# Modulation vectors finished four accumulators at a time instead of two, with six accumulator buffers

## The chip, the cores and the metric

The kernel runs on one core of one Trainium2 chip. The metric is the device time of one execution in microseconds (us); of several runs the median is given. The profiled execution is one further run of the same program.

## The reference

Two layers of a hybrid diffusion backbone run over 256 latent and 256 context tokens with 1024 channels. Each layer normalises its input, projects it into a short convolution, a Fourier mixer, an attention and three gates, merges the three branches, projects the sum, and adds a squared-ReLU MLP. Every normalised input and every residual is scaled by modulation vectors, which come from the conditioning vector `c` (latents) and `c_ctx` (context):

```python
for l in range(DEPTH):
    mod = (silu(c) @ w_mod[l] + b_mod[l])[:, None, :]            # 6 parts of 1024 numbers
    mod_c = (silu(c_ctx)[None] @ w_mod[l] + b_mod[l])[:, None, :]
    sh1, sc1, gt1, sh2, sc2, gt2 = split(mod, 6)
    h = modulate(x, g_norm1[l], sh1, sc1)                       # rms_norm(x, g) * (1 + scale) + shift
    z = h @ w_in[l]
    ...                                                         # convolution, Fourier, attention
    x = x + gt1 * merge_branches(z, ...)
    x = x + gt2 * sq_relu_mlp(modulate(x, g_norm2[l], sh2, sc2), w_ff1[l], w_ff2[l])
    # layer 0 does the same for the context tokens with mod_c
```

All inputs, weights and outputs are float32. `w_mod` is 2 x 1024 x 6144.

## The kernel before

**Matrix products.** Activations lie transposed: channels on the 128 partitions, tokens along the row (512 in layer 0, latents and context together; 256 in layer 1). Weights come in chunks of 1024 x 256 (`fetch`, line 384, one DMA from the queue of SP into one of two `raw` buffers). Each half of a chunk is split into a rounded part `whi` (cast on ACT, line 362) and a rest `wlo` (subtraction on DVE, line 363), four buffers each. `fm` (line 414) makes three matmuls per pair of tiles: high by high (line 437), low by high (440), high by low (442). One chunk of layer 0 is 48 matmuls with 512 columns and fills two of the four PSUM banks of the pool `mm`. A new chunk takes the two banks that are used longest ago, and can start when those have been read.

**The modulation vectors.** Parts 0 and 1 of layer 0 are computed at the start (`mod_start`) and aren't touched by the change. All others are side work that runs between the big products. `mod_loads` (line 270) loads `w_mod` in pieces of 256 rows x 512 columns into one of two `modr` buffers. `mod_steps` (line 312) multiplies each of 128 rows per partition by its number of `silu(c)` and adds it to an accumulator `acc` of 128 x 512 on DVE (line 327 the first time, then 329): eight such additions for one half part (512 of a part's 1024 columns) and one stream. In layer 0, and for parts 0 and 1 of layer 1, there are two streams (latent and context), so a half part fills two accumulators; for parts 2 to 5 of layer 1 it fills one.

What is left is a sum over the 128 partitions, which `mod_finish` (line 280) makes on TensorE when two accumulators are full. Four matmuls with 32 columns of ones as weights (line 286) each take 256 columns of an accumulator and write to a strip of 32 partitions of one PSUM tile. They are plain float32, of which the trace shows two records each. ACT copies the tile to SBUF (line 291), two transposes (line 296, of 128 x 128) bring the sums onto the partitions, and two small additions on DVE (line 299) add the bias and write `modT`. There are 16 such finishes.

**The order of the work.** `mod_steps` is a generator that is advanced one step at a time by `fm` (`mods.tick`, line 444), at a rate set per stage (`RATES`, line 35). Inside `mod_finish` it lets W1 steps pass ahead of the matmuls and W2 ahead of the transposes. `mod_need` (line 308) runs it on until a part is there, ahead of the code that uses the part: parts 2, 3 and 4 at the output projection (stage `wo`), part 5, which is the gate `gt2` of the MLP's residual, after the first block of hidden units in stage `ff`. From the program so recorded, a scheduler makes the order of each engine's instructions by a simulated timeline. Some instructions (`keep_in_program_order`) keep their order among themselves. The engines then run their lists in order and wait for each other by semaphores.

Stages are named in the tiles: `init`, `n1`, `u`, `conv`, `fou`, `qkv`, `gate` (with the attention beside it), `ag`, `wo`, `ff`, each for layer 0 and 1. A tile `ffL_mm` is a bank of stage `ff`, `ffL_acc` an accumulator made there (the norm's sum of squares has the name `acc` too, lines 158 to 163). `residual` (line 452) reads a bank, multiplies it by `gt` from `modT`, and adds it to `xT` on DVE (line 455).

Of the kernel before, what the change touches and what calls it, by code (L numbers as in the profile page):

```python
# [8 lines left out]
F32 = mybir.dt.float32  # L9
F32R = mybir.dt.float32r  # L10
AF = mybir.ActivationFunctionType
ALU = mybir.AluOpType
# [3 lines left out]
P = 128  # L16
D = 1024
KT = D // P
# [12 lines left out]
NT0 = 2  # L31
MLAG = 1
LAG = 2
W1, W2 = 3, 2
RATES = [0.6, 1.3, 0.4, 0.8]
AR = [1.3, 0.8]

# [2 lines left out]
def hybrid_block_kernel(  # L40
# [7 lines left out]
    nc = tc.nc  # L48
# [13 lines left out]
    pmod = ctx.enter_context(tc.tile_pool(name="pmod", bufs=1, space=PSUM))  # L62
# [4 lines left out]
    def nm(s):  # L67
        uid[0] += 1
        return f"{stage[0]}_{s}_{uid[0]}"
# [4 lines left out]
    def scratch(shape=(P, 512), dt=F32):  # L74
        return scr.tile(list(shape), dt, tag="scr", name=nm("scr"))

    def small(shape, tag, dt=F32, bufs=4):
        return tiny.tile(shape, dt, tag=tag, name=nm(tag), bufs=bufs)
# [4 lines left out]
    def aux(shape=(P, 512)):  # L83
        return paux.tile(list(shape), F32, tag="aux", name=nm("aux"))
# [34 lines left out]
    ones = const.tile([P, P], F32, tag="ones", name="ones")  # L119
# [7 lines left out]
    prm = []  # L127
# [103 lines left out]
    modT = [const.tile([P, 48, 2], F32, tag=f"modT{l}", name=f"modT{l}") for l in range(DEPTH)]  # L231
# [38 lines left out]
    def mod_loads(todo):  # L270
        for l, j, ns in todo:
            for h in range(2):
                for k2 in range(KT // 2):
                    r = tiny.tile([P, 2, 512], F32, tag="modr", name=nm("modr"), bufs=2)
                    c0 = j * D + h * 512
                    nc.sync.dma_start(r, w_mod[l, k2 * 256 : (k2 + 1) * 256, c0 : c0 + 512]
                                      .rearrange("(k p) n -> p k n", p=P))
                    yield l, j, ns, h, k2, r

    def mod_finish(accs, dsts, l):  # L280

        ps = pmod.tile([P, 256], F32, tag="mod", name=nm("mod"))
        for _ in range(W1):
            yield
        for g in range(4):
            tc.keep_in_program_order(PE.matmul(
                ps[32 * g : 32 * g + 32, :], ones[:, 0:32],
                accs[g // 2][:, (g % 2) * 256 : (g % 2 + 1) * 256], start=True, stop=True,
            ))
        sb = scratch()[:, :256]  # L290
        A.copy(sb, ps)
        for _ in range(W2):
            yield
        tp = aux((P, 2, P))
        for e in range(2):
            tc.keep_in_program_order(PE.transpose(tp[:, e, :], sb[:, e * P : (e + 1) * P], ident))
        tv = tp.rearrange("p e (g r) -> p g e r", r=32)[:, :, :, 0]
        for i, (f, s) in enumerate(dsts):
            V.tensor_tensor(
                modT[l][:, f : f + 4, s].rearrange("p (g e) -> p g e", e=2),  # L300
                tv[:, 2 * i : 2 * i + 2, :],
                prm[l][:, f : f + 4].rearrange("p (g e) -> p g e", e=2), op=ALU.add,
            )
        yield

    ready = set()
# [5 lines left out]
    def mod_steps(todo):  # L312
        loads = mod_loads(todo)
        cur = next(loads, None)
        accs, dsts = [], []
        while cur is not None:
            l, j, ns, h, k2, r = cur
            cur = next(loads, None)
            if k2 == 0:
                for s in range(ns):  # L320
                    accs.append(small([P, 512], "acc", bufs=2))
                    dsts.append((j * 8 + h * 4, s))
            for kk in range(2):
                for s in range(ns):
                    a, w = accs[s - ns], cs2[:, s, 2 * k2 + kk : 2 * k2 + kk + 1]
                    if k2 + kk == 0:
                        v = V.tensor_scalar(a, r[:, kk, :], w, None, op0=ALU.mult)
                    else:
                        v = V.scalar_tensor_tensor(a, r[:, kk, :], w, a, op0=ALU.mult, op1=ALU.add)  # L329
                    tc.keep_in_program_order(v)  # L330
                    yield
            if k2 == KT // 2 - 1 and len(accs) == 2:
                yield from mod_finish(accs, dsts, l)
                accs, dsts = [], []
                if h == 1:
                    ready.add((l, j))


    class Side:
# [3 lines left out]
        def set(self, gen, rate):  # L343
            self.gen, self.rate, self.due = gen, rate, 0.0
# [167 lines left out]
    for l in range(DEPTH):  # L512
# [3 lines left out]
        T = ns * S  # L516
# [115 lines left out]
        for tt in range(nt):  # L632
            ps = aux((P, 2, 256))
# [17 lines left out]
        for ft in range(2):  # L651
            ps = aux()
# [108 lines left out]
        for ci, c0 in ((2, OFF_K), (0, OFF_Q), (1, OFF_Q + 256)):  # L761
            ch = plain(w_in[l], 0, c0, (V, G) if last else (V, V)).prep()
            for tt in range(4 if ci == 2 else nt):
                ps = bank((P, 256))
# [126 lines left out]
        for j in range(4):  # L891
# [5 lines left out]
            for o in range(2):  # L897
                f = 2 * j + o
# [42 lines left out]
        acc = accs(streams)  # L941
# [4 lines left out]
        rbc = []  # L946
# [9 lines left out]

        def norm2(s, rb, todo):
            if last:
                rbc.append(small([P, 512], "acc", bufs=2)[:, :T])
                A.copy(rbc[0], rb)  # L960
                return
            modulate(hh2, hl2, todo, {s: rb}, gn2, sh2)

        project(lambda j: plain(w_o[l], 0, j * 256), msrc, gt1, acc, norm2)


# [25 lines left out]
        for b in range(nblk):  # L992
# [40 lines left out]
            if nr == 1:  # L1033
                if final and not last:
                    mods.drain()
                    acc = accs(streams)
# [88 lines left out]
```

## Time and profile before

| | before |
|---|---|
| median of 3 runs | 1148.34 us (1147.14 to 1148.45) |
| the profiled execution, its own time | 1147.6 us |
| span of the profiled execution | 1145.7 us |
| TensorE (PE), busy | 1123.6 us, 98% |
| DVE, busy | 779.8 us, 68% |
| ACT, busy | 503.2 us, 44% |
| DMA, all queues | 180.02 MB, mean 157 GB/s |

The 1.9 us between the profiled execution's time and its span lie before the first and after the last instruction. PE is busy nearly throughout. PE's matmuls overlap: one starts every 0.23 us and lasts 0.39, so that the distance from one start to the next, not the duration, says what a matmul costs. PEld is the queue of the weight loads, one ahead of each matmul; in brackets stands how long PE or PEld was idle ahead of a row, and for whom.

### The profile page before, as it was taken

The numbers are of one execution on the slowest core, as the hardware profiler recorded it, in microseconds if no ns is written. First come the engines' busy times: TensorE is split into PE (matmuls) and PEld (weight loads), VectorE is DVE, ScalarE is ACT, GpSimd is POOL, SyncE is SP. The second block draws the span as 40 slices with busy tenths as digits, with TensorE's granted clock in tenths as the row PEclk, the third lists the DMA queues.
The fourth block names the chain that finished last, engine by engine and source line by source line (L and its number), as shares of the span: only waits on it lengthen the run. The fifth ranks groups of instructions, "written<-read, shape, count | busy, mean of one in ns | idle before, by whom it ended". The sixth has DMA issues, their size and how long they took to land.

```text
span 1145.7 us, 17784 instructions
## 1 busy us (share of the span) xinstructions
PE 1123.6 (98%) x7083; PEld 980.9 (86%) x7083; DVE 779.8 (68%) x1434; ACT 503.2 (44%) x884; POOL 59.1 (5%) x57
## 2 busy tenths in 40 slices
PE   6999999999999999999999999999999999999998
PEld 4689888887787998878888888899999999988986
DVE  4677776577878876766656664678886567756754
ACT  4245444443332454243234135245666456754652
POOL 2102100000000100000000000033300000000000
PEclk9999999999999999999999999999999999999999
DMA  9923322234755253655456664525434565555553
GB/s 291 293 90 98 93 92 82 86 110 120 205 172 184 82 173 115 198 174 178 130 177 208 206 209 141 198 78 167 147 111 130 137 202 178 182 184 184 184 184 110
DMA packets 156764, 180.02 MB, mean 157 GB/s; under 512 B 5229, under 2 KB 126473, under 8 KB 156681
## 3 DMA queue, kind: packets, MB, share of 16 engines
q1 hardware_dynamic: 156680, 178.88, 49.9%
q8 instruction: 56, 0.92, 0.3%
q14 instruction: 28, 0.22, 0.1%
HBM read 177.81 MB, written 1.05 MB: 156 GB/s over the span
## 4 chain that ended last, share of the span: by engine, by line
PE 90%; SPq 3%; DMA 3%; DVE 2%; ACT 1%; POOL 0%; issue 0%; DVEq 0%; ACTq 0%
PE ffL_mm L437 12%; PE ffL_mm L440 12%; PE ffL_mm L442 12%; PE gateL_mm L437 5%; PE gateL_mm L440 5%; PE gateL_mm L442 5%; PE agL_mm L440 3%; PE agL_mm L437 3%; PE agL_mm L442 3%; PE ffL_mm L1070 3%; PE ffL_mm L1071 3%; PE ffL_mm L1069 3%; SPq L468 2%; PE woL_mm L440 2%; PE woL_mm L442 2%; PE woL_mm L437 2%
## 5 line engine op out<-in xcount | busy, mean ns | idle before, releaser
L362 ACT CAST ffL_whi<-ffL_raw 128x1024 fp32r<-128x1024 f32 x128 | 134.4, 1052 | 217.9 <-PE ffL_mm L442 164.1
L363 DVE TENSOR_TENSOR ffL_wlo<-ffL_raw,ffL_whi 128x1024 fp32r<-128x1024 f32 x127 | 155.2, 1222 | 100.4 <-ACT ffL_whi L362 100.2
L437 PE MATMUL ffL_mm<-woL_big,ffL_whi 128*128 128x258 f32 (+2 forms) x544 | 171.1, 329 | 0.0
L440 PE MATMUL ffL_mm<-woL_big,ffL_wlo 128*128 128x258 f32 (+2 forms) x544 | 170.5, 327 | 0.0
L442 PE MATMUL ffL_mm<-woL_big,ffL_whi 128*128 128x258 f32 (+2 forms) x544 | 133.2, 328 | 0.0
L437 PEld LDWEIGHTS ffL_mm<-woL_big,ffL_whi 128*128 128x128 f32 x544 | 103.0, 190 | 10.2 <-issue 1.6
L440 PEld LDWEIGHTS ffL_mm<-woL_big,ffL_wlo 128*128 128x128 f32 x544 | 103.1, 190 | 8.9 <-issue 0.4
L329 DVE SCALAR_TENSOR_TENSOR ffL_acc<-ffL_modr,cs,ffL_acc 128x512 f32<-128x512 f32 x126 | 90.5, 748 | 25.6 <-DMA ffL_modr<-in_w_mod_dram 24.6
L437 PE MATMUL ffL_mm<-ffL_big,ffL_whi 128*128 128x512 f32 (+1 forms) x288 | 105.3, 368 | 0.0
L440 PE MATMUL ffL_mm<-ffL_big,ffL_wlo 128*128 128x512 f32 (+1 forms) x288 | 104.9, 367 | 0.0
L442 PEld LDWEIGHTS ffL_mm<-woL_big,ffL_whi 128*128 128x128 f32 x544 | 91.0, 190 | 8.7
L442 PE MATMUL ffL_mm<-ffL_big,ffL_whi 128*128 128x512 f32 (+1 forms) x288 | 85.0, 367 | 0.0
L437 PEld LDWEIGHTS ffL_mm<-ffL_big,ffL_whi 128*128 128x128 f32 x288 | 54.3, 189 | 10.6 <-issue 2.1
L440 PEld LDWEIGHTS ffL_mm<-ffL_big,ffL_wlo 128*128 128x128 f32 x288 | 54.3, 189 | 9.0 <-issue 0.4
L363 DVE TENSOR_TENSOR gateL_wlo<-gateL_raw,gateL_whi 128x1024 fp32r<-128x1024 f32 x40 | 48.9, 1222 | 19.2 <-ACT gateL_whi L362 17.5
L442 PEld LDWEIGHTS ffL_mm<-ffL_big,ffL_whi 128*128 128x128 f32 x288 | 53.1, 189 | 8.7
L437 PE MATMUL gateL_mm<-n1L_big,gateL_whi 128*128 128x512 f32 x128 | 50.6, 397 | 0.0
L440 PE MATMUL gateL_mm<-n1L_big,gateL_wlo 128*128 128x512 f32 x128 | 50.3, 393 | 0.0
L1069 PE MATMUL ffL_mm<-ffL_whi,ffL_big 128*128 128x512 f32 x128 | 49.9, 390 | 0.0
L1070 PE MATMUL ffL_mm<-ffL_wlo,ffL_big 128*128 128x512 f32 x128 | 49.8, 389 | 0.0
L1071 PE MATMUL ffL_mm<-ffL_whi,ffL_big 128*128 128x512 f32 x128 | 49.8, 389 | 0.0
L362 ACT CAST gateL_whi<-gateL_raw 128x1024 fp32r<-128x1024 f32 x40 | 42.0, 1050 | 17.1 <-PE gateL_mm L442 11.9
(335 smaller groups left out, 2628.1 us busy)
## 6 DMA issues: line engine op xcount, KB each, us to landing
ffL_raw<-in_w_ff_dram SPq DMA_DIRECT2D x64, 1024.0 KB, 5.4
ffL_modr<-in_w_mod_dram SPq DMA_DIRECT2D x53, 512.0 KB, 5.1
gateL_raw<-in_w_in_dram SPq DMA_DIRECT2D x16, 1024.0 KB, 5.3
init_big<-in_w_mod_dram SPq DMA_DIRECT2D x16, 512.0 KB, 7.8
agL_raw<-in_w_in_dram SPq DMA_DIRECT2D x8, 1024.0 KB, 5.4
woL_raw<-in_w_o_dram SPq DMA_DIRECT2D x8, 1024.0 KB
qkvL_raw<-in_w_in_dram SPq DMA_DIRECT2D x6, 1024.0 KB
agL_modr<-in_w_mod_dram SPq DMA_DIRECT2D x11, 512.0 KB, 3.7
```

The costliest lines, as they stand in the source:

```text
L329: v = V.scalar_tensor_tensor(a, r[:, kk, :], w, a, op0=ALU.mult, op1=ALU.add)
L362: a = A.copy(hi[:, :n], src)
L363: b = eng.tensor_tensor(lo[:, :n], src, hi[:, :n].bitcast(F32), op=ALU.subtract)
L437: m = PE.matmul(d, wh, rh, start=kt == first, stop=False)
L440: PE.matmul(d, wl, rh, start=False, stop=False)
L442: PE.matmul(d, wh, rl, start=False, stop=kt == final)
L468: nc.sync.dma_start(t[:, f, i], w_mod[0, :, c0 : c0 + P].rearrange("(k p) n -> p k n", p=P))
L1069: PE.matmul(bs[tt], hid[:, 0], wh, start=kk == 0, stop=False)
L1070: PE.matmul(bs[tt], hid[:, 0], wl, start=False, stop=False)
L1071: PE.matmul(bs[tt], hid[:, 1], wh, start=False, stop=kk == nk - 1)
```

## The change

A finish now takes four accumulators. Each of its four matmuls takes a whole accumulator of 512 columns to its strip of 32 partitions, so the PSUM tile has 512 columns; the copy on ACT has 512 columns, the transposes are four and the additions four, of [128, 4] as before. There are 8 finishes instead of 16. Six accumulators may be alive instead of two. The waits inside a finish become W1 = W2 = 4 steps. A part counts as ready with its finish: with two streams one finish is one part, with one stream it is two parts. The number of additions of line 329, the loads of `w_mod` and their sizes stay as they are. The larger accumulator pool (8 KB more per partition) is paid for by a smaller reserve for dynamic transfers (`dynamic_dma_scratch_size=1024`); the kernel's loads and stores go through SP's queue q1, and beside it the profile names only queues for instructions.

```diff
-W1, W2 = 3, 2
+W1, W2 = 4, 4
...
     def mod_finish(accs, dsts, l):
-        ps = pmod.tile([P, 256], F32, tag="mod", name=nm("mod"))
+        ps = pmod.tile([P, 512], F32, tag="mod", name=nm("mod"))
         for _ in range(W1):
             yield
         for g in range(4):
             tc.keep_in_program_order(PE.matmul(
-                ps[32 * g : 32 * g + 32, :], ones[:, 0:32],
-                accs[g // 2][:, (g % 2) * 256 : (g % 2 + 1) * 256], start=True, stop=True,
+                ps[32 * g : 32 * g + 32, :], ones[:, 0:32], accs[g], start=True, stop=True,
             ))
-        sb = scratch()[:, :256]
+        sb = scratch()
         A.copy(sb, ps)
         for _ in range(W2):
             yield
-        tp = aux((P, 2, P))
-        for e in range(2):
+        tp = aux((P, 4, P))
+        for e in range(4):
             tc.keep_in_program_order(PE.transpose(tp[:, e, :], sb[:, e * P : (e + 1) * P], ident))
-        tv = tp.rearrange("p e (g r) -> p g e r", r=32)[:, :, :, 0]
-        for i, (f, s) in enumerate(dsts):
+        for g, (f, s) in enumerate(dsts):
             V.tensor_tensor(
-                modT[l][:, f : f + 4, s].rearrange("p (g e) -> p g e", e=2),
-                tv[:, 2 * i : 2 * i + 2, :],
-                prm[l][:, f : f + 4].rearrange("p (g e) -> p g e", e=2), op=ALU.add,
+                modT[l][:, f : f + 4, s], tp[:, :, 32 * g], prm[l][:, f : f + 4], op=ALU.add
             )
...
-                    accs.append(small([P, 512], "acc", bufs=2))
+                    accs.append(small([P, 512], "acc", bufs=6))
...
-            if k2 == KT // 2 - 1 and len(accs) == 2:
+            if k2 == KT // 2 - 1 and len(accs) == 4:
                 yield from mod_finish(accs, dsts, l)
+                ready.update((l, f // 8) for f, _ in dsts)
                 accs, dsts = [], []
-                if h == 1:
-                    ready.add((l, j))
...
-    nc = bacc.Bacc("TRN2", target_bir_lowering=False, num_devices=1)
+    nc = bacc.Bacc("TRN2", target_bir_lowering=False, num_devices=1, dynamic_dma_scratch_size=1024)
```

The order of the instructions changes at the finishes and around them. Line numbers of the change are up to 5 smaller from line 299 on (299 is 297, 437 is 432, 442 is 437, 455 is 450).

**First place: the residual of the first MLP block in layer 0, which needs part 5.** Before, DVE finishes the first half of part 5 (the rows of line 299), works on the accumulators `ffL_acc_4320` and `4321` of the second half, and reaches the residuals of the first chunk's banks, `ffL_mm_4363` and `4364`, in between:

```order
L299 TENSOR_TENSOR modT_120<-ffL_aux_4313,prm_110 128x4
L327 TENSOR_SCALAR ffL_acc_4320<-ffL_modr_4214,cs_105 128x512 [waits DMAHW7_49]
...
L329 SCALAR_TENSOR_TENSOR ffL_acc_4321<-ffL_modr_4318,cs_105,ffL_acc_4321 128x512 [waits DVE_49]
...
L455 SCALAR_TENSOR_TENSOR xT<-ffL_mm_4363,modT_120,xT 128x256 [waits PE_49]
...
L455 SCALAR_TENSOR_TENSOR xT<-ffL_mm_4364,modT_120,xT 128x256 [waits PE_49]
...
L329 SCALAR_TENSOR_TENSOR ffL_acc_4320<-ffL_modr_4326,cs_105,ffL_acc_4320 128x512 [waits DMAHW4_49,DVE_49]
```

Now DVE has both halves to finish before any residual. In the list of DVE the residuals of the first two chunks (banks `4331`, `4332`, `4404`, `4405`) stand behind the one finish and two first accumulations:

```order
L325 SCALAR_TENSOR_TENSOR ffL_acc_4247<-ffL_modr_4296,cs_105,ffL_acc_4247 128x512 [waits DVE_49]
L358 TENSOR_TENSOR ffL_wlo_4555<-ffL_raw_4550,ffL_whi_4554 128x1024 [waits DMAHW4_49,Activation_49]
L297 TENSOR_TENSOR modT_120<-ffL_aux_4315,prm_110 128x4 [waits PE_49]
L297 TENSOR_TENSOR modT_120<-ffL_aux_4315,prm_110 128x4 x3
L323 TENSOR_SCALAR ffL_acc_4326<-ffL_modr_4302,cs_105 128x512 [waits DMAHW6_49]
L323 TENSOR_SCALAR ffL_acc_4327<-ffL_modr_4302,cs_105 128x512
L450 SCALAR_TENSOR_TENSOR xT<-ffL_mm_4331,modT_120,xT 128x256 [waits DVE_49] x2
L450 SCALAR_TENSOR_TENSOR xT<-ffL_mm_4332,modT_120,xT 128x256 x2
```

On PE the transposes of that finish now stand at the end of the second chunk, right ahead of the third, whose first bank `ffL_mm_4478` is the one that `4331` had:

```order
L437 MATMUL ffL_mm_4404<-ffL_big_4128,ffL_whi_4439 128x512
L437 MATMUL ffL_mm_4405<-ffL_big_4128,ffL_whi_4439 128x512
L295 MATMUL ffL_aux_4315<-ident,ffL_scr_4313 128x128 [waits Activation_49]
L295 MATMUL ffL_aux_4315<-ident,ffL_scr_4313 128x128 x3
L432 MATMUL ffL_mm_4478<-ffL_big_3891,ffL_whi_4480 128x512 [waits DVE_49,PE_49]
L435 MATMUL ffL_mm_4478<-ffL_big_3891,ffL_wlo_4481 128x512
```

What moved: the one place where part 5 becomes known lies after the second chunk instead of inside the first and the third, and the third chunk's first matmul waits for DVE.

**Second place: transposes that follow their sums at once.** Before, PE has the matmuls of a finish, its transposes and the first product of stage `ag` in a row at the end of stage `gate` of layer 0:

```order
L442 MATMUL gateL_mm_2816<-convL_big_674,gateL_whi_2798 128x512
L286 MATMUL gateL_mod_2696<-gateL_acc_2233,ones 32x256 [waits DVE_49]
L286 MATMUL gateL_mod_2696<-gateL_acc_2233,ones 32x256
L286 MATMUL gateL_mod_2696<-gateL_acc_2234,ones 32x256 [waits DVE_49]
L286 MATMUL gateL_mod_2696<-gateL_acc_2234,ones 32x256
L296 MATMUL gateL_aux_2767<-ident,gateL_scr_2743 128x128 [waits Activation_49]
L296 MATMUL gateL_aux_2767<-ident,gateL_scr_2743 128x128
L437 MATMUL agL_mm_2840<-n1L_big_188,agL_whi_2842 128x512 [waits Activation_49]
```

Now that row of things is gone there, and a like one stands inside stage `ag`, ahead of its last gate chunk:

```order
L437 MATMUL agL_mm_3182<-qkvL_big_893,agL_whi_3183 128x512
L286 MATMUL agL_mod_3040<-agL_acc_2911,ones 32x512 [waits DVE_49]
L286 MATMUL agL_mod_3040<-agL_acc_2912,ones 32x512 [waits DVE_49]
L295 MATMUL agL_aux_3118<-ident,agL_scr_3082 128x128 [waits Activation_49]
L295 MATMUL agL_aux_3118<-ident,agL_scr_3082 128x128 x3
L432 MATMUL agL_mm_3228<-n1L_big_188,agL_whi_3230 128x512 [waits Activation_49]
```

What moved: in both rows PE needs ACT's copy for the transposes and ACT's next instructions for a bank; the place changed and the copy is twice as wide.

Counted over the whole list of PE, the matmuls of line 286 stood in 21 unbroken groups before (11 finishes in one group, 5 in two) and stand in 15 now: four finishes in one group, two in two groups of two matmuls each, one in three groups and one in four groups of a single matmul. The last finish stood before inside the last block's projection of layer 0 (its two groups apart); it now stands right ahead of that projection.

More of the change, by code (lines that the diff above doesn't have):

```diff
@@ L958, in norm2 @@
             if last:
-                rbc.append(small([P, 512], "acc", bufs=2)[:, :T])
+                rbc.append(small([P, 512], "acc", bufs=6)[:, :T])
                 A.copy(rbc[0], rb)
```

## The prediction

> **What bounds the kernel now.** I read the page first: the shares and the chain that ended last.
>
> ```profile
> span 1145.7 us, 17784 instructions
> PE 1123.6 (98%) x7083; PEld 980.9 (86%) x7083; DVE 779.8 (68%) x1434; ACT 503.2 (44%) x884; POOL 59.1 (5%) x57
> PE 90%; SPq 3%; DMA 3%; DVE 2%; ACT 1%; POOL 0%; issue 0%; DVEq 0%; ACTq 0%
> ```
>
> TensorE (PE) has the end. Next came the windows, to see in which stretch PE has idle time at all (columns: stretch and its length, busy time and instructions of PE, PEld, DVE, ACT, POOL, granted clock, DMA share, GB/s).
>
> ```profile
> 60.00:740.00 680.00, 679.10 (x3670) 567.04 (x3669) 470.52 (x832) 261.80 (x452) 15.25 (x17) 1.00 0.47 147
> 740.00:800.00 60.00, 56.69 (x468) 55.50 (x468) 49.26 (x92) 29.27 (x59) 21.19 (x14) 1.00 0.38 117
> 800.00:1140.00 340.00, 340.00 (x2534) 322.05 (x2533) 225.66 (x409) 190.72 (x338) 10.65 (x9) 1.00 0.52 163
> ```
>
> In 680 us PE idles 0.9 us, between 740 and 800 it idles 3.3 us, after that nothing. So a change of the modulation sums counts by two things only: what its own matmuls cost between the big products, and which waits of PE it makes or removes. DVE and ACT, at 68% and 44%, count only where PE waits for them. Because matmuls overlap, the cost is read from distances between starts, in the timeline.
>
> **The change part by part.** The sums are made against the profiled execution's own 1147.6 us; the median, 1148.34, lies 0.74 above it.
>
> *The sums on PE (line 286).* First a whole group of a finish (x8: four matmuls, two records each) between two matmuls of a product, then a group of half a finish (x4).
>
> ```profile
> 588.71 0.39 PE L440 MATMUL ffL_mm<-woL_big,ffL_wlo 128*128 128x512 f32 x1
> ...
> 589.39 0.61 PE L442 MATMUL ffL_mm<-woL_big,ffL_whi 128*128 128x512 f32 x2
> 589.94 0.64 PE L286 MATMUL ffL_mod<-ffL_acc,ones 128*32 128x256 f32 x8
> 590.51 0.50 PE L437 MATMUL ffL_mm<-woL_big,ffL_whi 128*128 128x512 f32 x1
> 590.84 0.39 PE L440 MATMUL ffL_mm<-woL_big,ffL_wlo 128*128 128x512 f32 x1
> ...
> 187.81 0.63 PE L442 MATMUL gateL_mm<-n1L_big,gateL_whi 128*128 128x512 f32 x2
> 188.37 0.63 PE L286 MATMUL gateL_mod<-gateL_acc,ones 128*32 128x256 f32 x4
> ...
> 189.26 0.40 PE L440 MATMUL gateL_mm<-n1L_big,gateL_wlo 128*128 128x512 f32 x1
> ```
>
> From 589.39 to 590.84 PE starts three product matmuls (two of line 442, one of 437) and the group in 1.45 us. Between 588.71 and 589.39 three start (the two left out are of lines 437 and 440), one each 0.227 us. So the group costs 1.45 - 3 x 0.227 = 0.77. The half group costs 189.26 - 187.81 - 0.68 = 0.77 too. Four strips cost what two cost, so the strips run beside each other. Before, there are 21 groups: 16.2 us. Now there are 15. Halving the finishes doesn't halve the groups, since a finish's four matmuls stand apart more often. Each new matmul has 512 columns instead of 256. What that costs shows in the durations of the groups (mean ns of one behind the busy time):
>
> ```profile
> L437 PE MATMUL ffL_mm<-woL_big,ffL_whi 128*128 128x512 f32 x224 | 87.9, 392 | 0.0
> L437 PE MATMUL ffL_mm<-woL_big,ffL_whi 128*128 128x256 f32 x64 | 16.0, 284 | 0.0
> L286 PE MATMUL ffL_mod<-ffL_acc,ones 128*32 128x256 f32 x72 | 6.4, 391 | 1.1 <-DVE ffL_acc L329 1.1
> ```
>
> For a product, 256 columns more are 108 ns more. A record of line 286 with 256 columns lasts as long as a product's with 512, so it streams its columns twice, and 256 columns more are 2 x 108 = 216 ns. There are two records one after the other on each strip: a group becomes 0.77 + 0.43 = 1.20 us. 15 x 1.20 - 16.2 = **+1.8 us**. The weight queue gives the same from other rows (in brackets its idle time ahead of a row, which is the rest of a group's price):
>
> ```profile
> 589.93 0.16 PEld L286 LDWEIGHTS ffL_mod<-ffL_acc,ones 128*32 128x32 f32 x8 [0.35 <-issue]
> 590.50 0.19 PEld L437 LDWEIGHTS ffL_mm<-woL_big,ffL_whi 128*128 128x128 f32 x1 [0.41 <-issue]
> ...
> 53.12 0.81 PEld L251 LDWEIGHTS n1L_mod<-init_big,init_scr 128*32 128x32 f32 x32 [0.35 <-issue]
> 54.13 0.19 PEld L437 LDWEIGHTS n1L_mm<-n1L_big,n1L_whi 128*128 128x128 f32 x1 [0.20 <-issue]
> ```
>
> The group of line 251, from the start of the program, has eight records of 128 columns on each strip, twice the columns of a group of line 286, as the new one will have. It takes 1.01 us from its first load to the next product's, where line 286 takes 0.57: 0.44 more. With that a group costs 1.21 and the term is +2.0, the upper end. The lower end is -4.6, if a group costs 0.77 whatever its columns (15 x 0.77 = 11.6). I take +1.8; two ways of reading agree on it, and the lower end contradicts both.
>
> *The first MLP block of layer 0 (lines 450 and 455).* Part 5 was known after one half group at a time; PE never waited there: the row at 463.20 has DVE waiting for PE, not the reverse.
>
> ```profile
> 446.42 0.38 PE L296 MATMUL ffL_aux<-ident,ffL_scr 128*128 128x128 f32 x2
> ```
>
> ```profile
> 446.84 0.23 DVE L299 TENSOR_TENSOR modT<-ffL_aux,prm 128x4 f32<-128x4 f32 x2 [1.06 <-PE ffL_aux L296]
> 446.99 0.87 DVE L327 TENSOR_SCALAR ffL_acc<-ffL_modr,cs 128x512 f32<-128x512 f32 x2
> ...
> 463.20 1.66 DVE L455 SCALAR_TENSOR_TENSOR xT<-ffL_mm,modT,xT 128x256 f32<-128x256 f32 x4 [1.09 <-PE ffL_mm L442]
> ```
>
> Now PE's list has the transposes of part 5 right ahead of the third chunk, whose first matmul waits for DVE to have read its bank. Behind the transposes DVE has in its list four additions (two took 0.23; two more, at 0.08, make 0.4), two TENSOR_SCALARs of the next part (0.87) and two of the residual's instructions (1.66 / 2 = 0.83). The bank is free 2.1 us after the transposes end; with the signals between engines (0.04 from 446.80 to 446.84, and a like or larger one back, then PE's refill) I take **+2.3 us**. Nothing hides it: PE's list has nothing between. What could lengthen it is the data of the TENSOR_SCALAR, which waits for a load:
>
> ```profile
> DVE ffL_acc L327 <- DMA ffL_modr<-in_w_mod_dram: 4.9, 3, 2.5
> ```
>
> Its longest wait was 2.5, so the upper end is +4.8; the lower is +1.4, if the TENSOR_SCALARs (0.87) don't stand in the way. Behind this residual DVE has the other banks' and the third chunk's `wlo`; PE, late by as much, gives DVE the time back.
>
> *The wait at 742 us goes.* The last group of layer 0 stood in the last block's projection and waited for the last accumulation:
>
> ```profile
> 742.12 0.14 PEld L286 LDWEIGHTS ffL_mod<-ffL_acc,ones 128*32 128x32 f32 x4 [1.25 <-DVE ffL_acc L329]
> ```
>
> Round an undisturbed group PEld idles 0.35 (above), so 0.9 of the 1.25 was waiting. The finish now stands ahead of that projection, its accumulations earlier in DVE's list: **-0.9** (other end 0, if it waits there). In place of it the tail's own waits are next, which I cover below.
>
> *Transposes and copies (296, 291).* There are 32 transposes before and after, in 8 groups instead of 16.
>
> ```profile
> 471.73 0.40 PE L442 MATMUL ffL_mm<-ffL_big,ffL_whi 128*128 128x512 f32 x1
> 471.96 0.39 PE L296 MATMUL ffL_aux<-ident,ffL_scr 128*128 128x128 f32 x2
> ...
> 472.43 0.39 PE L437 MATMUL ffL_mm<-ffL_big,ffL_whi 128*128 128x512 f32 x1
> ```
>
> Two product matmuls (at 471.73 and 472.11) and two transposes (one matmul's pair of records) take 0.70, so the transposes cost 0.70 - 0.45 = 0.25. At the same price per transpose nothing changes; the second matmul's longer spacing (0.32 instead of 0.23) is paid once per group and is saved eight times at most, -0.7. I take **-0.3**.
>
> At the end of stage `gate` of layer 0 PE waits for the copy:
>
> ```profile
> 274.30 0.16 PEld L286 LDWEIGHTS gateL_mod<-gateL_acc,ones 128*32 128x32 f32 x8 [0.36 <-issue]
> ...
> 276.27 0.19 PEld L437 LDWEIGHTS agL_mm<-n1L_big,agL_whi 128*128 128x128 f32 x1 [0.30 <-ACT gateL_scr L857]
> ```
>
> ```profile
> 275.36 0.36 ACT L291 COPY gateL_scr<-gateL_mod 128x256 f32<-128x256 f32 x1
> 275.62 1.09 ACT L857 ACTIVATE gateL_scr<-gateL_mm 128x512 f32<-128x512 f32 x2
> ```
>
> The group's own 0.57 (589.94 to 590.51) ends at 274.87; 1.40 us later the next product starts. Now this sequence is gone here and a like one stands in stage `ag`, with a copy of 512 (an ACT instruction of 512 took 1.09 / 2 = 0.54 instead of 0.36) but without the ACTIVATE behind it: **0**, ends -0.5 and +1.1 (one such pair ahead of it on ACT).
>
> *The attention.* In PE's list the attention's 64-wide products (line 820) now stand in 14 unbroken groups instead of 13, since the side work falls elsewhere among them:
>
> ```profile
> 183.75 1.73 PEld L820 LDWEIGHTS gateL_aux<-qkvL_big,qkvL_vt 128*64 128x64 f32 x32 [0.36 <-issue]
> 185.64 0.30 PEld L793 LDWEIGHTS gateL_aux<-qkvL_kT,qkvL_big 128*128 128x128 f32 x2 [0.17 <-issue]
> ```
>
> One group more idles 0.36 + 0.17 = **+0.5** (0 to 1.0).
>
> *The change of layers.* Three waits on DVE are left there:
>
> ```profile
> 766.63 0.74 PE L442 MATMUL n1L_mm<-ffL_big,n1L_whi 128*128 128x256 f32 x4 [0.29 <-DVE ffL_big L207]
> 770.24 0.68 PE L198 MATMUL ffL_aux<-ffL_scr,ones 128*128 128x128 f32 x4 [0.71 <-DVE ffL_scr L197]
> 786.10 0.38 PE L410 MATMUL fouL_aux<-fouL_whi,fouL_big 128*128 128x256 f32 x1 [1.26 <-DVE fouL_big L450]
> ```
>
> None is for a sum, and DVE has the same accumulations: **0**, with -2.3 (all three) as the end if side work moved out of their way.
>
> Six accumulators instead of two let DVE go on while a finish waits; DVE isn't the bound, so it gains nothing but cover: 0. The groups of one or two matmuls in stages `wo` and `ff` could each wait for an accumulation, as at 742 (0.9 each, five places: up to +4.5); DVE has idle time there, so I take 0.
>
> Sum: 1.8 + 2.3 - 0.9 - 0.3 + 0.5 = +3.4. The profiled execution would take 1147.6 + 3.4 = 1151.0 us, the median 1148.34 + 3.4 = **1151.7 us**.
>
> **The rivals.**
>
> *A group costs its switch, not its columns (faster).* The half and the whole group both cost 0.77, and 0.76 of idle time (0.35 + 0.41) stands round one in the weight queue. If the columns run inside that idle time, 15 groups cost 11.6 us and the first term is -4.6 instead of +1.8: 3.4 - 6.4 = -3.0, or 1145.3 us. It decides where 512 columns still fit into the time that 256 take. Against it stands the 391 ns of a record. The Trainium skill, TensorEngine Tiling (Array Packing), section Key Properties, says that changing the tiling mode drains TensorE; the idle time on both sides of the 32-column weights agrees. By that rule alone only the number of groups would count, and the change would come out as this rival has it.
>
> *The third chunk doesn't wait.* If the bank's residual is done early (by another order of bank reuse than I read), the +2.3 goes: +1.1, 1149.4 us, no measurable change. For it: before, nothing waited there. Against: DVE's list has the residual behind the transposes, and PE's has them right ahead of the chunk.
>
> *The groups apart wait for DVE.* Each wait as at 742: up to 3.4 + 4.5 = +7.9, with half of them +5.6: 1154.0 us. For it: 742 itself. Against: six buffers, and idle time of DVE of 32%.
>
> **How the numbers follow.** The forecast has 0.55, the first rival 0.12, the second 0.13, the third 0.12, and mixtures with smaller gains at the change of layers 0.08. A measurement of this kernel can tell about 0.2%, 2.3 us, from no change: 1146.0 and 1150.6 are the bounds. The forecast alone, with its smaller terms' ends, spans 1149.5 to 1154; a fifth of it is under 1150.6. Slower: 0.44 of the forecast and 0.12 of the third rival, less 0.01, 0.55. Same: 0.11 + 0.13 + 0.05 of the first rival's partial form + 0.05 of the mixtures, 0.34. Faster: the rest, 0.11. The range leaves out the first rival's full form and the worst of the third: 1147.0 to 1155.5.
>
> **What would show it.** In the changed kernel's timeline: a group of line 286 should lengthen the spacing of product matmuls by 1.20 instead of 0.77 (right) or stay at 0.77 (first rival). In stage `ff` of layer 0, first block, the first matmul of the third chunk should have an idle time of some 2 us put down to DVE's `xT` (line 450); without such a row the second rival holds. No row of line 286 should show an idle time over 0.4 us on PEld put down to DVE; rows that do, summed, are the third rival. PE's idle time between 60 and 740 us should rise from 0.9 to about 3. A time under 1147 us would make the forecast wrong whatever the rows say.

## The result and the profile after

The changed kernel takes 1162.49 us (median of 6 runs) against 1148.39 us (median of 6): a ratio of 1.0122, 95% interval 1.0107 to 1.0137, or 14 us more. The forecast was 1151.7, with a range up to 1155.5. The sign was right and the size wrong by a factor of four. The profiled execution took 1160.96 us. First its page:

```profile
span 1159.2 us, 17622 instructions
PE 1128.2 (97%) x7019; PEld 982.2 (85%) x7019; DVE 780.3 (67%) x1434; ACT 502.4 (43%) x876; POOL 58.3 (5%) x57
```

PE's busy time has grown by 4.6 us, the span by 13.5; DVE and ACT do the same work as before. So most of the loss is PE standing still (and part of the busy time is a slower clock, below). The windows over the same stretches say where:

```profile
60.00:740.00 680.00, 670.90 (x3555) 556.22 (x3555) 467.91 (x831) 258.74 (x445) 15.25 (x17) 1.00 0.46 146
740.00:800.00 60.00, 56.73 (x438) 54.71 (x437) 39.61 (x75) 25.48 (x46) 14.26 (x11) 1.00 0.34 106
800.00:1140.00 340.00, 340.00 (x2587) 324.42 (x2586) 233.39 (x425) 194.65 (x349) 16.73 (x12) 1.00 0.53 167
```

Between 60 and 740 us PE idled 0.9 us before; now it is 9.1. Layer 1 is untouched. What PE waited for, from the view of waits (total, times, longest; waits of the program's start left out):

```profile
PE ffL_mm L437 <- DVE ffL_big L445: 4.4, 1, 4.4
...
PE ffL_mm L432 <- DVE xT L450: 2.1, 1, 2.1
PE agL_aux L295 <- ACT agL_scr L290: 1.7, 1, 1.7
PE fouL_aux L405 <- DVE fouL_big L445: 1.7, 1, 1.7
...
PE ffL_aux L198 <- DVE ffL_scr L197: 1.3, 1, 1.3
PE gateL_aux L788 <- ACT qkvL_big L794: 0.8, 1, 0.8
```

The first, second, third and last of these rows, 9.0 us together, are the 9.1; the other two lie at the change of layers. The second row is the wait at the third chunk that the prediction has. The last is in the attention of stage `gate`: ACT has a finish's copy ahead of the exponential that PE waits for. The first was in no part of the prediction. It stands alone in PE's timeline, and what comes behind it belongs to it:

```profile
638.54 0.39 PE L435 MATMUL ffL_mm<-ffL_big,ffL_wlo 128*128 128x512 f32 x1
643.37 0.73 PE L437 MATMUL ffL_mm<-ffL_big,ffL_whi 128*128 128x512 f32 x2 [4.44 <-DVE ffL_big L445]
643.93 0.43 PE L432 MATMUL ffL_mm<-ffL_big,ffL_whi 128*128 128x512 f32 x1
644.17 0.62 PE L435 MATMUL ffL_mm<-ffL_big,ffL_wlo 128*128 128x512 f32 x1
644.59 0.63 PE L432 MATMUL ffL_mm<-ffL_big,ffL_whi 128*128 128x512 f32 x1
645.02 0.63 PE L435 MATMUL ffL_mm<-ffL_big,ffL_wlo 128*128 128x512 f32 x1
...
647.58 0.40 PE L435 MATMUL ffL_mm<-ffL_big,ffL_wlo 128*128 128x512 f32 x1
```

After the wait, product matmuls start every 0.43 us instead of 0.227, until 647.58: the clock was about half. The window says so as well:

```profile
640.00:650.00 10.00, 6.63 (x22) 5.32 (x23) 8.21 (x12) 1.04 (x1) 0.00 (x0) 0.83 0.78 254
```

A granted clock of 0.83 over 10 us is 1.7 us lost on top of the 4.44. The Trainium skill, page TensorE: Matmul & The Clock Gate, section What's actually happening, says that an idle window of about 3.4 us puts the array to half rate and about 3.4 us of work brings it back; the 3.4 us of half-rate starts here (644.17 to 647.58) agree.

What did PE wait for? DVE's timeline around it (line 445 is the subtraction that makes the low part of the squared ReLU, line 325 an accumulation of the modulation sums; in brackets DVE's idle time):

```profile
633.94 0.75 DVE L325 SCALAR_TENSOR_TENSOR ffL_acc<-ffL_modr,cs,ffL_acc 128x512 f32<-128x512 f32 x1
636.72 1.54 DVE L325 SCALAR_TENSOR_TENSOR ffL_acc<-ffL_modr,cs,ffL_acc 128x512 f32<-128x512 f32 x2 [2.04 <-DMA ffL_modr<-in_w_mod_dram]
639.00 1.54 DVE L325 SCALAR_TENSOR_TENSOR ffL_acc<-ffL_modr,cs,ffL_acc 128x512 f32<-128x512 f32 x2 [0.74 <-DMA ffL_modr<-in_w_mod_dram]
...
641.96 0.75 DVE L325 SCALAR_TENSOR_TENSOR ffL_acc<-ffL_modr,cs,ffL_acc 128x512 f32<-128x512 f32 x1 [0.28 <-DMA ffL_modr<-in_w_mod_dram]
642.63 1.28 DVE L445 TENSOR_TENSOR ffL_big<-ffL_scr,ffL_big 128x512 fp32r<-128x512 f32 x2
```

ACT had finished its side of that tile here:

```profile
632.63 1.14 ACT L444 CAST ffL_big<-ffL_scr 128x512 fp32r<-128x512 f32 x2
```

ACT was done at 633.77; DVE subtracts at 642.63, 8.9 us later. In between, its list has accumulations that wait for loads of `w_mod`. The delay had grown over the run of accumulations that began at 593.8: the same step came 0.9 us after ACT's cast at 602.01, 4.6 at 616.65, 7.1 at 630.01 and 8.9 here. Before the change it was at most 1.6 us in the same block. In the block's first three chunks the delay costs PE nothing; in the last one PE waits 4.44 us, 4.42 less than the delay of 8.86. The same difference comes back in every profile that has this wait (e1: 9.17 and 4.75; e3: 9.64 and 5.22; e7: 8.37 and 3.94; e10: 8.48 and 4.07). So PE has 4.4 us in hand there, and pays for what goes beyond.

The theory: the change makes the one-stream parts of layer 1 come in runs of 32 accumulations without a pause, where it was 16. A one-stream part uses a load of 512 KB for two accumulations; with two load buffers the loads can't keep the pace, DVE falls behind by 2 to 4 us per chunk, and the subtraction of line 445 stands behind the late accumulations in DVE's list. Late loads are not new: before the change DVE waited 24.6 us for them, all told.

```profile
DVE ffL_acc L329 <- DMA ffL_modr<-in_w_mod_dram: 24.6, 16, 3.8
```

What would be new is that the delays add up over a longer run. The rivals: an accident of one execution; DVE running ahead because of the two spare accumulators; a full DMA queue, whatever the buffers.

### The profile page after: what moved, and what is told of

It is laid out like the page before. It is cut to its first block, busy times and chain, and to the rows that moved or that the text cites. A ratio compares the mean times of both kernels' runs of the same rounds, so it can differ in the third digit from the quotient of the medians.

```text
span 1159.2 us, 17622 instructions
## 1 busy us (share of the span) xinstructions
PE 1128.2 (97%) x7019; PEld 982.2 (85%) x7019; DVE 780.3 (67%) x1434; ACT 502.4 (43%) x876; POOL 58.3 (5%) x57
## 4 chain that ended last, share of the span: by engine, by line
PE 88%; DMA 4%; SPq 3%; DVE 2%; ACT 1%; issue 0%; POOL 0%; DVEq 0%; ACTq 0%
PE ffL_mm L432 12%; PE ffL_mm L437 12%; PE ffL_mm L435 11%; PE gateL_mm L432 5%; PE gateL_mm L435 5%; PE gateL_mm L437 5%; PE agL_mm L432 3%; PE agL_mm L437 3%; PE agL_mm L435 3%; PE ffL_mm L1066 3%; PE ffL_mm L1065 3%; PE ffL_mm L1064 3%; DMA ffL_modr<-in_w_mod_dram 2%; SPq L463 2%; PE woL_mm L435 2%; PE woL_mm L432 2%
## 5 line engine op out<-in xcount | busy, mean ns | idle before, releaser
L325 DVE SCALAR_TENSOR_TENSOR ffL_acc<-ffL_modr,cs,ffL_acc 128x512 f32<-128x512 f32 x126 | 90.8, 748 | 33.8 <-DMA ffL_modr<-in_w_mod_dram 32.9
```

## The experiments

Times are medians, each beside runs of the kernel before on the same chip. Positions along the kernel are compared by the time of the same product matmul in two profiles.

**e1: the change once more**, no edit.

> The changed kernel once more, unaltered. Its first profile had one PE wait of 4.44 us in the MLP of layer 0 (line 437 for DVE's line 445) and, right behind it, some 13 product matmuls at 0.42 us instead of 0.23. Theory 1 (a wait built into the order of DVE's list and the pace of the w_mod loads): it is there again, 3 to 6 us at the same instruction, with the slow matmuls behind it, and the time is 12 to 16 us over before. Theory 2 (an accident of that one execution): the wait is absent or under 1 us, and the time is 5 to 8 us over before.

1163.02 us against 1149.12, ratio 1.0125 (1.0110 to 1.0139). The wait is there, 4.75 us at the same instruction. An accident is excluded. The wait at the third chunk is there too, and this time it also halves the clock behind it:

```profile
470.00:480.00 10.00, 7.88 (x30) 6.13 (x29) 7.88 (x19) 1.05 (x1) 0.00 (x0) 0.83 0.06 12
640.00:650.00 10.00, 5.25 (x18) 3.87 (x17) 7.74 (x12) 0.74 (x1) 0.00 (x0) 0.83 0.76 244
```

In the first profile the window 470 to 480 had a clock of 1.00 with the same 2.1 us wait. So one wait of 2 us costs 2.1 us in one execution and 3.8 in the next; this may be a part of the spread of the changed kernel (1159.4 to 1166.5).

**e2: a third buffer for the loads.** Two accumulators fewer pay for it. (The other places that draw on these two pools have the same numbers.)

```diff
-r = tiny.tile([P, 2, 512], F32, tag="modr", name=nm("modr"), bufs=2)
+r = tiny.tile([P, 2, 512], F32, tag="modr", name=nm("modr"), bufs=3)
...
-accs.append(small([P, 512], "acc", bufs=6))
+accs.append(small([P, 512], "acc", bufs=4))
```

> The changed kernel with three buffers for the loads of w_mod instead of two, and four accumulators instead of six (same memory). PE has the same groups of line 286. Theory 1 (DVE's accumulations wait for loads that come late because a load can start only when one of two buffers is read, and the subtraction of line 445 stands behind them): the wait of 4.4 us at line 437 shrinks to under 1.5 us, the slow clock behind it goes, the time falls by 4 to 7 us against the changed kernel. Rival (the queue is full, the loads are late whatever the buffers): the wait stays at 3 us or more and the time within 2 us of the changed kernel's. The wait at the third chunk of the first block (2.1 us) stays in both.

1154.54 us, ratio 1.0057 (1.0043 to 1.0071): 8.5 us below e1, more than the 4 to 7 expected. Between the two profiles, e2 gains 6.5 us from 630 to 660 us, which are the wait and its clock; another 3.3 us are there by 630 us, most of it from two things: the clock stays up behind the third chunk's wait in this execution (1.7), and the wait in `ag` is 0.7 us instead of e1's 2.1, as it is in e9, the other kernel of this finish with three load buffers. In PE's view of waits no row of line 437 for `ffL_big` L445 is left; the groups of line 286 are 15 as in the change. DVE's side shows why:

```profile
633.91 0.75 DVE L325 SCALAR_TENSOR_TENSOR ffL_acc<-ffL_modr,cs,ffL_acc 128x512 f32<-128x512 f32 x1 [3.08 <-DMA ffL_modr<-in_w_mod_dram]
634.58 1.22 DVE L358 TENSOR_TENSOR ffL_wlo<-ffL_raw,ffL_whi 128x1024 fp32r<-128x1024 f32 x1
635.71 0.75 DVE L325 SCALAR_TENSOR_TENSOR ffL_acc<-ffL_modr,cs,ffL_acc 128x512 f32<-128x512 f32 x1
636.37 1.29 DVE L445 TENSOR_TENSOR ffL_big<-ffL_scr,ffL_big 128x512 fp32r<-128x512 f32 x2
```

The same subtraction comes at 636.37 instead of 642.63, 3.9 us after ACT's cast: DVE is still behind, but by less than the 4.4 us that PE has in hand. DVE's waits of line 325 on these loads went from 32.9 us in 19 waits to 14.0 in 6:

```profile
DVE ffL_acc L325 <- DMA ffL_modr<-in_w_mod_dram: 14.0, 6, 3.9
```

```profile
DVE ffL_acc L325 <- DMA ffL_modr<-in_w_mod_dram: 32.9, 19, 4.3
```

(the first of e2, the second of the changed kernel). The queue isn't full: between 593 and 645 us it moved more with three buffers (251 GB/s) than with two:

```profile
593.00:645.00 52.00, 52.00 (x231) 43.07 (x230) 38.04 (x52) 21.77 (x34) 0.00 (x0) 1.00 0.75 251
```

```profile
593.00:645.00 52.00, 47.56 (x208) 38.98 (x208) 36.37 (x53) 20.62 (x32) 0.00 (x0) 0.99 0.69 220
```

(again e2 first, then the changed kernel; here PE stands still for 4.4 us of the 52.)

**e10: the other half of e2's edit**, four accumulators and two load buffers.

```diff
-accs.append(small([P, 512], "acc", bufs=6))
+accs.append(small([P, 512], "acc", bufs=4))
```

> The changed kernel with four accumulators instead of six, and two load buffers as in the change: the part of e2 that isn't the third load buffer. Theory 1 (the load buffers decide): the wait of 4.4 us stays at 3 us or more with slow matmuls behind it; 1160 to 1166 us. Rival (the two spare accumulators let DVE run ahead of the loads, and e2 was faster for that): the wait is under 1.5 us and the time is at 1154 to 1157 us.

1161.70 us, ratio 1.0114 (1.0100 to 1.0129). The wait is there (4.07 us) with a clock of 0.83 in 640 to 650 us. So what took the wait away in e2 is the load buffer, not DVE being held back.

**e4: one-stream parts finished by two**, so that their accumulations come in runs of 16. (Here, in e3, e7, e9 and e11, a finish of two also makes copy and transposes take only the rows that are filled, and marks its part as ready with the second half.)

```diff
-            if k2 == KT // 2 - 1 and len(accs) == 4:
+            if k2 == KT // 2 - 1 and len(accs) == (2 if ns == 1 else 4):
```

> The changed kernel, but the parts with one stream (2 to 5 of layer 1) are finished two accumulators at a time, so that their accumulations come in runs of 16 with a pause, as before the change; parts with two streams stay at four. Theory 1 (runs of 32 accumulations, each pair with a load of its own, outrun the loads; a pause every 16 lets them catch up): the wait of 4.4 us is under 1.5 us and the slow clock goes; four more groups of 1.2 us are paid; together 1 to 3 us less than the changed kernel. Rival (the length of the runs doesn't matter): the wait stays above 3 us and the time rises by 4 to 5 us.

1159.84 us, ratio 1.0106 (1.0089 to 1.0122): 3.2 below e1, at the edge of what was expected. The 4.4 us wait and its slow clock are gone, with two load buffers. Instead 18 groups of line 286 are paid. The subtraction is 4.9 us late at 617.24, near the end of the first 16 accumulations, much as in the changed kernel; behind the finish's pause DVE has caught up, and the next one, at 622.76, follows ACT's cast at once. So shorter runs with a pause between them keep the delay from growing, as the theory has it. More finishes also bring more pauses, so e4 doesn't part the length of a run from the pause.

**e8: the side work at 0.7 steps per tick**, runs of 32 as in the change.

```diff
-RATES = [0.6, 1.3, 0.4, 0.8]
+RATES = [0.6, 1.3, 0.4, 0.7]
```

> The changed kernel with the side work advanced 0.7 steps per tick instead of 0.8 in the MLP (RATES). Two load buffers as in the change. Theory 1 (the pace of the accumulations outruns the loads): 12% fewer accumulations per us, so the lag at the end of a run shrinks and the wait of 4.4 us falls under 2 us, without slow matmuls behind it; three more groups of line 286 (18 instead of 15) cost up to 3.6 us; the time is 1 to 5 us below the changed kernel's. Rival (the place of the accumulations in DVE's list decides, not the pace): the wait stays at 3 us or more and the time rises.

1164.80 us, ratio 1.0139 (1.0125 to 1.0153). Half a hit: the wait at line 437 is gone. The run of 32 lies over the same chunks (600.8 to 662 us), DVE still waits for its loads, but the subtractions follow ACT's casts at once. The run also begins some 6 us later against the chunks than in the changed kernel, so e8 doesn't part the pace from the place. And the time rose. The side work isn't done by the end of layer 0, and PE waits there:

```profile
PE ffL_aux L198 <- DVE ffL_scr L197: 4.3, 1, 4.3
```

That is 1.3 in the changed kernel; the clock falls behind it too (0.79 and 0.87 in the two windows from 770 to 790 us). The product matmul that the kernel before has at 761 us is 18.7 us later here, and 12.6 us later in the changed kernel.

**e3: part 5 of layer 0 in halves**, so that the third chunk needn't wait; four accumulators otherwise.

```diff
-            if k2 == KT // 2 - 1 and len(accs) == 4:
+            if k2 == KT // 2 - 1 and len(accs) == (2 if (l, j) == (0, 5) else 4):
```

> The changed kernel, but part 5 of layer 0 is finished in two halves of two accumulators each (two matmuls with 512 columns each). That gives one finish more. Theory: the wait of 2.1 us at the third chunk's first matmul is under 0.5 us; one group more costs 1.2 us and the transposes about the same; the time falls by 0.5 to 1.5 us. Rival (that wait only moves to the next thing that needs part 5): a wait of 1.5 us or more stays in the first block and the time doesn't fall.

1163.65 us, ratio 1.0125 (1.0110 to 1.0140). The wait for `xT` is gone from the view, but the time didn't fall: 17 groups stand in PE's order instead of 15, which at 1.2 us eat the 2.1, and one finish more has four transposes more (some 0.6 us); the wait at line 437 was 5.2 us in this execution. The expected gain was missed because the sum counted one group more, not two.

**e7: the same kernel a second time**, a single run (its label names a load buffer that the kernel doesn't have).

> The kernel of e3 a second time, one look: the changed kernel with part 5 finished in halves, two buffers for the loads. The wait in the MLP of layer 0 is there again, 4 to 6 us, and the third chunk of the first block shows no wait over 0.5 us.

The wait at line 437 is there, 3.9 us, just under what was expected, and the third chunk's isn't. 1160.82 us.

**e9: both cures**, three load buffers and part 5 in halves.

> The kernel of e2 (three load buffers, four accumulators) with part 5 of layer 0 finished in halves, as in e3. Theory: both waits are gone, that of 4.4 us and that of 2.1 us at the third chunk; one more finish is paid (one or two groups of 1.2 us); against e2 (1154.5) the time falls by 0 to 1.5 us, to about 1153.7. Rival (the 2.1 us at the third chunk had been hidden by what PE waits for later): the time rises by the new group's 1.2 to 2.4 us.

1154.73 us, ratio 1.0059 (1.0046 to 1.0072), the same as e2's 1154.54. Both waits are gone and nothing is gained over e2: again two groups more for a 2.1 us wait less. This is between what the theory and the rival had.

**e5 and e6: the finish of before with the new pools.** e5 has six accumulators and the smaller reserve, e6 four accumulators, three load buffers and the smaller reserve.

```diff
-accs.append(small([P, 512], "acc", bufs=2))
+accs.append(small([P, 512], "acc", bufs=6))
...
-nc = bacc.Bacc("TRN2", target_bir_lowering=False, num_devices=1)
+nc = bacc.Bacc("TRN2", target_bir_lowering=False, num_devices=1, dynamic_dma_scratch_size=1024)
```

> The kernel before with only the pools of the change: six accumulator buffers and the smaller reserve for dynamic transfers; finishes of two accumulators as before. Theory: the pools cost nothing, time within 2 us of before, the 21 groups stay, and the 1.05 us wait at 742 us shrinks or stays. Rival (the buffers let DVE run ahead into late loads, and that makes the 4.4 us wait): a PE wait of over 2 us in the MLP of layer 0, and 4 us or more over before. It also tells whether the first 62 us, 1.2 to 1.9 us longer in all five profiles of changed kernels than in the one of before, come with the pools (then they are longer here too) or differ from run to run.

> The kernel before with three buffers for the loads of w_mod, four accumulators and the smaller reserve; finishes as before. Theory: with two streams or runs of 16 the loads did not hold PE before the change, so nothing is to be gained but the 1.05 us wait at 742 us: 0 to 1.5 us faster than before. Rival (late loads cost PE time before the change too, hidden in the rows): over 2.3 us faster.

e5: 1148.15 against 1149.11, ratio 0.9993 (0.9984 to 1.0002). e6: 1148.92, ratio 1.0003 (0.9994 to 1.0011). The pools are neutral, and with the old finish a third load buffer has nothing to gain: in e6 the wait at 742 us shrank to 0.34 us, but 0.6 came back at line 198. The start is a matter of the execution: up to 62 us, e5 and e7 were as fast as the profile of before (0.0 and 0.1 us later), the first profile of the change 1.5 us later, the others 0.9 to 2.5, whichever kernel.

**e11 and e12: the counterpart, and the pauses alone.** e11 finishes the two-stream parts by two and the one-stream parts by four (`2 if ns == 2 else 4`); e12 has W1, W2 = 3, 2 with everything else as in the change.

> The changed kernel, but the parts with two streams are finished two accumulators at a time and only the parts with one stream by four: the counterpart of e4. Theory 1: the wait of 4.4 us, which lies in the run of one-stream parts, is there (3 us or more, if those runs still fall into the MLP blocks), the waits at the third chunk (2.1 us) and in stage ag (1.7 us) are gone; 1156 to 1162 us. Rival (the four-accumulator finishes of the two-stream parts push the later runs into the wrong place): the 4.4 us wait is gone, and the time is within 4 us of before.

> The changed kernel with the pauses inside a finish as before (W1 = 3, W2 = 2 instead of 4 and 4). Theory 1: the runs of 32 accumulations stay and the pauses are shorter, so the loads have less time to catch up; a wait of 3 us or more stands in the MLP of layer 0, at this or another instruction; 1160 to 1167 us. Rival (the longer pauses put the run where it hurts): no such wait, 1152 to 1157 us.

e11: 1170.87 us, ratio 1.0194 (1.0180 to 1.0209), outside what either theory had. It has no wait at line 437, but 25 groups of line 286: ten more than the change, at 1.2 us each 12 us. Twenty of them hold a single matmul, and a single one costs as much as four do. Six finishes more also bring 24 transposes more, some 4 us (four transposes lengthen the product's spacing by 0.45 us in the changed kernel, most of those here by 0.59). From e1's 1163.0, with these 16 and with 3.8 for a wait of 2.3 us for ACT's `woL_big` at 407 us and the clock of 0.85 behind it, and less what is gone of e1's waits, 6.5 (line 437), 3.8 (third chunk), 1.4 (`ag`), 0.8 (attention) and 1.0 (the change of layers), it would be 1169.3; the other 1.6 us are open. It doesn't test the runs of 32: the later half of the first such run, with 13.5 us of waits for loads, now lies behind the block's last subtraction (653.9 to 682.9 us).

e12: 1159.75 us, ratio 1.0099 (1.0085 to 1.0113). The wait at line 437 that the theory expected isn't there, and the time is what neither had; but the delay is there. DVE is 2.0, 4.0 and 5.7 us behind ACT in the block's first three chunks, and 4.5 in the last:

```profile
638.59 1.14 ACT L444 CAST ffL_big<-ffL_scr 128x512 fp32r<-128x512 f32 x2
```

```profile
644.25 1.29 DVE L445 TENSOR_TENSOR ffL_big<-ffL_scr,ffL_big 128x512 fp32r<-128x512 f32 x2
```

```profile
644.49 0.39 PE L435 MATMUL ffL_mm<-ffL_big,ffL_wlo 128*128 128x512 f32 x1
644.99 0.73 PE L437 MATMUL ffL_mm<-ffL_big,ffL_whi 128*128 128x512 f32 x2
```

From 644.88 to 644.99 PE stands still for 0.11 us, which is 4.52 less 4.42 once more. The run begins 3 us earlier than in the changed kernel, on chunks that come 6 us later, so its end weighs less on the last subtraction. What e12 pays instead is 1.9 us for an accumulation and 1.2 us for ACT in stage `gate`, with a slow clock behind (0.71 in 270 to 280 us). So a run of 32 makes DVE late; whether PE pays depends on where the run lies against the block's last subtraction, and this shifts with every number of the side work.

## Why the prediction was wrong, by its own steps

Position by position, the changed kernel's profile is later than that of before by 1.5 us at 62 us, 5.3 at 440, 9.7 at 490, 8.1 at 630, 15.9 at 660, 12.6 at 747 and 13.5 at the end.

**What PE's own work costs: right.** A group of line 286 in the changed kernel:

```profile
584.01 0.61 PE L437 MATMUL ffL_mm<-ffL_big,ffL_whi 128*128 128x512 f32 x2
584.55 1.06 PE L286 MATMUL ffL_mod<-ffL_acc,ones 128*32 128x512 f32 x8
585.55 0.50 PE L432 MATMUL ffL_mm<-woL_big,ffL_whi 128*128 128x512 f32 x1
585.88 0.39 PE L435 MATMUL ffL_mm<-woL_big,ffL_wlo 128*128 128x512 f32 x1
```

1.87 us for three product matmuls (0.68) and the group: 1.19, forecast 1.20. So +1.8 for the first term holds, and the first rival, that only the switch counts, is out: columns are paid in full.

**The third chunk: right.** 2.13 us of idle time, released by `xT`, forecast 2.3, so the second rival is out. DVE did what the order said:

```profile
471.72 0.37 DVE L297 TENSOR_TENSOR modT<-ffL_aux,prm 128x4 f32<-128x4 f32 x4 [6.00 <-PE ffL_aux L295]
472.01 0.87 DVE L323 TENSOR_SCALAR ffL_acc<-ffL_modr,cs 128x512 f32<-128x512 f32 x2
472.80 2.83 DVE L450 SCALAR_TENSOR_TENSOR xT<-ffL_mm,modT,xT 128x256 f32<-128x256 f32 x7
```

What it lacked: in e1, e8, e10 and e12 this same wait of 2.1 us is followed by a halved clock, some 1.7 us more.

**The wait at 742 us: right** (gone, -0.9). **Separate groups waiting for DVE: right** that they don't; the changed kernel's view of PE's waits has no row of line 286, so the third rival is out too.

**The transposes: nearly right.** Between products, two cost 0.23 us before and four cost 0.45 now, so nothing is saved: 0 instead of -0.3. **The attention: right in the groups, short by a wait.** There are 14 groups instead of 13, as forecast, but the wait of 0.8 us for ACT at line 788 was in no term.

**Transposes in stage `ag`: mis-sized.** I took 0 with +1.1 as the upper end. The group starts at 328.56 and takes 0.99; the next product starts at 331.84, 2.29 us later, where it was 1.40: +0.9.

```profile
328.56 1.05 PE L286 MATMUL agL_mod<-agL_acc,ones 128*32 128x512 f32 x4
331.34 0.66 PE L295 MATMUL agL_aux<-ident,agL_scr 128*128 128x128 f32 x4 [1.73 <-ACT agL_scr L290]
331.84 0.50 PE L432 MATMUL agL_mm<-n1L_big,agL_whi 128*128 128x512 f32 x1
```

ACT has a cast of 1.04 us at 329.75 ahead of the copy, so the +1.1 of the upper end was near, though the instruction ahead of the copy is another than the one I had named. **The change of layers: mis-sized**, 3.3 us of waits instead of 2.3: +1.0, with 0 taken.

**The step that failed** is the one that took DVE's side as unchanged: "DVE has the same accumulations: 0", and the sum's silence about any PE wait behind them. The number of accumulations is the same, but not when they come. (The "it gains nothing but cover: 0" on the six buffers held as far as it went: e5 has them with the old finish and is level, and e10 has the wait with four.) I never looked at how fast `w_mod` can arrive for a run of 32, though the waits for these loads were in view: 24.6 us of them on line 329 before the change, and 2.5 us in the row that I used for the third chunk. A subtraction behind the accumulations in DVE's list, on which PE has 4.4 us in hand, wasn't priced at all. It cost 4.4 us and 1.7 us of clock, 6.1 in all, and a halved clock behind a wait was in no term either. With the 0.9 in `ag`, the 0.8 in the attention, the 1.0 at the change of layers and the 1.5 us at the start (which other executions don't have), 3.4 + 10.3 = 13.7 stand against the 13.5 us between the two profiles. And e2, where the long wait is absent, is 5.9 us later than before at its last product matmuls, 1.2 of it by 62 us. The other 4.7 stand against the forecast's 3.4, the 1.0 at the change of layers and the 0.8 in the attention (its wait in `ag` is 0.7, so that term fits there). So where the late subtraction costs PE nothing, the kernel of the four-accumulator finish lies inside the forecast's range (1154.54 us), near its upper end.

No version beats the kernel before: the best of the four-accumulator kernels is 5.4 us behind, and the pools without the new finish are level.

## What to carry to other kernels

When side work on a shared in-order engine is regrouped, count not only how much of it there is but how long it comes without a pause, and set its pace against its loads and their buffers: the step behind it in the same list waits with it. A finish that is wider saves nothing on TensorE where columns and not instructions are paid. And a gap on TensorE of about 2 us or more should be priced with the slow matmuls that may follow it: in these runs mostly 1.7 us more.

## What was not expected of the hardware

The 2.1 us wait at the third chunk halved the clock for some 3.5 us in four profiles (e1, e8, e10, e12) and left it alone in three (the first, e2, e4). A wait of 1.9 us in e12 (stage `gate`) and one of 2.3 us in e11 lowered it too, while the waits of 1.5 to 2.1 us in `ag` (the first, e1, e3, e4, e7, e8, e10) never did. Waits of 3.9 us and more at lines 437 and 198 lowered it in all six (the first, e1, e3, e7, e8, e10). By the rule of the page TensorE: Matmul & The Clock Gate of the Trainium skill, section What's actually happening, an idle window of about 3.4 us does this; the cases of 1.9 to 2.3 us show that a shorter gap can be enough, in some executions. The same section says that the window runs free of the kernel, which would explain that it differs from run to run; no run here shows the window itself.
